# Two more blocks of the modulation matrix summed row by row during the scan, handed out with its projections

## The chip, the cores and the metric

The kernel runs on one core of a Trainium2 chip. The metric is the device time of one execution in microseconds; lower is better. Engines are named as in the profile: PE (TensorE matmuls), PEld (its weight loads), DVE (VectorE), ACT (ScalarE), POOL (GpSimd) and SP (SyncE, which here only issues DMAs). Each engine works through its own list of instructions in a fixed order, and waits at an instruction until what it needs is there.

## The reference

One layer of a diffusion trunk on 512 latent tokens and 256 context tokens, model width 2048, in float32:

```
mod  = silu(c) @ w_ada + b_ada                 # 6 x 2048 columns: sh1 sc1 gt1 sh2 sc2 gt2
p    = modulate(rms_norm(x, g_mix), sh1, sc1) @ w_in       # the context alike, with c_ctx
f    = fourier_mix(p[:, :512], w_fourier)
y    = ssd_mixer(p_ctx[:, 512:], p[:, 512:], ...)          # conv, two scans, gate, grouped norm
x    = x + gt1 * (concat(f, y) @ w_out)
x    = x + gt2 * (relu(modulate(rms_norm(x, g_mlp), sh2, sc2) @ w_mlp1)**2 @ w_mlp2)
out  = rms_norm(x, g_final)
```

The change concerns the 12288 columns of `mod`, held in the tile `mod` as 96 columns of 128 values: 0 to 15 are sh1, 16 to 31 sc1, 32 to 47 gt1, 48 to 63 sh2, 64 to 79 sc2, 80 to 95 gt2. sh2 and sc2 are needed only after the output projection.

## The kernel before, in words

Each large product keeps weights of 128 x 1024 as a tile `wraw` that is split into `whi` (ACT, rounded to the fast float format) and `wlo` (DVE, the rest), and does three matmuls for each piece (`mm3`, L106 to L108): high weights with high input, low weights with high input, high weights with low input. In the scan and the output projection `load_split` issues the load on SP (L98) and makes both halves (L99, L100), with three buffers for `wraw` and two for each half. A w_in or w_out product (`product`) has two such tiles, 48 matmuls of 512 columns.

The columns of `mod` are made in two ways.

- `ada_half` (L168 to L173): one column of 128 values from half a row at a time. A 512 KB load of transposed weights (`araw<-in_w_ada`, SP) and one multiply-and-sum over 1024 elements on DVE (L172, with a short read of the accumulator), with the conditioning vector spread over all partitions in `cl` or `clb`. Two of them for a column.
- `ada_rest` (L188 to L207): four columns, a block of 512, from rows. Eight steps; a step loads 512 KB (`araw<-in_w_adr`, L194, SP) and adds two rows of 128 x 512 to a sum `adacc` on DVE (L198 for the first, L200). After the eighth step four small matmuls (L204) sum over partitions and turn the block into columns, and DVE adds the bias (L206).

`NSB` says where the two meet: blocks 8 to `NSB` - 1 and 20 to 23 go by rows, the rest by columns. Blocks 8 to 11 are summed while the context is worked on, 20 to 23 during the MLP. Blocks 12 to `NSB` - 1 are put in the list `todo` at the scan's start (with two load buffers, pool `sbg`, and one sum, `sbg1`), and the columns from 4 x `NSB` to 79 at the output projection's start. `background(n)` does the next n steps of the list at the places where it is called:

- `scan_group` (four groups of heads) calls `background(1)` after each of its three parts; in the last group it empties the list ahead of `z_last`, which makes the last three z tiles from `w_zs`.
- `lat_group(g, nbg)` makes the five projections of a group (B, three of x, C), with `background(nbg)` after each. Projections of group g + 1 are written behind the scan of group g.
- The output projection calls `background((21 - NSB) // 2)` after each of its 16 products.

The written order is not the order on the engines: a scheduler orders the instructions of each engine when the kernel is built, by priorities and its own costs, with the weight loads at a high priority. Matmuls of a scan group therefore stand among those of the next group's projections.

At the end of the last group these steps meet. The three z tiles are gated (L586), squared and summed (L592), summed over partitions by a matmul with ones (L696), and the group's norm (L154 to L158) scales the last three outputs (L700). The other thirteen inputs of the output projection lie in DRAM; `between` reloads them through the two buffers `cvr` (L717, POOL) and splits each into `bh` (ACT, L708) and `bl` (DVE, L709). PE meanwhile does k = 0 to 12 of the first three products (their accumulators are `first`), and the last three k when the last outputs are split. `clb`, 1 MB, is loaded by POOL (L759) into memory that the scan gives back, so after the last L700.

In the output projection a product ends with an add to x (L790), a square (L771) and a sum of squares (L772), and the result goes to DRAM.

Of the kernel before, what the change touches and what calls it, by code (L numbers as in the profile page):

```python
# [30 lines left out]
NL = L // 2 + 1  # L31
SLAB_IN = 944
NZ0 = 3
NSB = 14
SHARED = [(16 + k, 0) for k in range(2, 14)]
NZ1 = 9
N1P = 3
# [17 lines left out]
def tile_hybrid_trunk(ctx, tc, xT, ctxT, cvec, ccol, vec, alog, w_ada, w_adr, w_ins, w_zs, w_in, w_dt, w_f, w_o,  # L55
# [18 lines left out]
    def acc(n=L):  # L74
        return psa.tile([P, L], F32, name="acc")[:, :n]
# [12 lines left out]
    def raw_tile():  # L88
        return pools["wp"].tile([P, HALF], F32, name="wraw")
# [20 lines left out]
    def product(ps, src, x, cuts=(8, 16)):  # L110
        k0 = 0
        nk = len(x)
        for k1 in cuts:
            w = load_split(src[:, k0:k1], (k1 - k0) * src.shape[2], src.shape[2])
            for k in range(k0, k1):
                mm3(ps, (w[0][:, k - k0], w[1][:, k - k0]), x[k], k == 0, k == nk - 1)
            k0 = k1
# [47 lines left out]
    def ada_half(pool, ch, hf, *sums):  # L165

        a = pool.tile([P, HALF], F32, name="araw")
        nc.sync.dma_start(out=a, in_=w_ada[ch if ch < 32 else ch - (4 * NSB - 32), :, hf * HALF:(hf + 1) * HALF])  # L168
        for i, (dst, half, cond) in enumerate(sums):
            o = a if i == len(sums) - 1 else pools["ws"].tile([P, HALF], F32R, name="whi").bitcast(F32)  # L170
            first, last = vcol(V_BADA + ch), half[:, ch:ch + 1]
            v.tensor_tensor_reduce(o, a, cond[:, hf * HALF:(hf + 1) * HALF], 1.0, last if hf else first,  # L172
                                   ALU.mult, ALU.add, dst[:, ch:ch + 1] if hf else last)  # L173
# [11 lines left out]
    def ada_rest(ci, pool, pool1, name="adacc"):  # L185

        held = {}

        def step(k2):
            if k2 == 0:  # L190
                held["a"] = pool1.tile([P, 512], F32, name=name)
            a = held["a"]
            w = pool.tile([P, 2, 512], F32, name="araw") if pool else raw_tile().rearrange("p (a b) -> p a b", b=512)
            nc.sync.dma_start(out=w, in_=w_adr[ci - 8 if ci < NSB else ci - 20 + NSB - 8, k2])  # L194
            for j in range(2):
                k = 2 * k2 + j
                if k == 0:
                    v.tensor_scalar(a, w[:, j], cs[:, 0:1], None, ALU.mult)  # L198
                else:
                    v.scalar_tensor_tensor(a, w[:, j], cs[:, k:k + 1], a, ALU.mult, ALU.add)  # L200
            if k2 == 7:
                pt = bank()
                for j in range(4):
                    te.matmul(pt[:, 2 * j:2 * j + 2], a[:, j * P:(j + 1) * P], ones[:, 0:2], start=True, stop=True)  # L204
                sl = slice(ci * 4, ci * 4 + 4)
                v.tensor_add(mod[:, sl], pt[:, 0:8].rearrange("p (a b) -> p a b", b=2)[:, :, 0], vt[:, sl])  # L206
        return [lambda k2=k2: step(k2) for k2 in range(8)]  # L207
# [69 lines left out]
    def background(n):  # L277
        for _ in range(min(n, len(todo))):
            todo.pop(0)()
# [183 lines left out]
    def conv(ps, t, row, o, raw):  # L463
        s.copy(raw, ps)
        ps = raw
        s.activation(o, ps, AF.Identity, bias=vcol(V_CB + t), scale=vcol(V_CW + t * 5 + 2))
        ar = o.rearrange("p (r c) -> p r c", c=row)
        pr = ps.rearrange("p (r c) -> p r c", c=row)
        for j in (0, 1, 3, 4):
            off = j - 2  # L470
            if off < 0:
                o_, i_ = ar[:, :, -off:], pr[:, :, :row + off]
            else:
                o_, i_ = ar[:, :, :row - off], pr[:, :, off:]
            v.scalar_tensor_tensor(o_, i_, vcol(V_CW + t * 5 + j), o_, ALU.mult, ALU.add)
        s.activation(o, o, AF.Silu)

    def to_tok(src, n, dst):
        pt = bank()
        for c in range(n // P):  # L480
            te.transpose(pt[:, c * P:(c + 1) * P], src[:, c * P:(c + 1) * P], ident)
        s.copy(dst, pt[:, :n].rearrange("p (c q) -> p c q", q=P))

    def lat_group(g, nbg, extra=None):
        def proj(t, o):
            ps = acc()
            product(ps, w_in[t], xm)
            conv(ps, t - T_X, 64, o, gp2.tile([P, L], F32, name="cvr"))
            background(nbg)
            return o  # L490
        bT = proj(T_B + g, gp1.tile([P, L], F32, name="bT"))
        b_tok = gp2.tile([P, NCH, P], F32, name="b_tok")
        to_tok(bT, L, b_tok)
        if extra:
            extra()
        x_tok = gp2.tile([P, NCH, HG * 64], F32, name="x_tok")
        xs_ = []
        for i in range(3):
            o = proj(T_X + g * 3 + i, gp2.tile([P, L], F32, name=f"xT{i}"))
            to_tok(o, L, x_tok[:, :, i * P:(i + 1) * P])  # L500
            xs_.append(o)
        cT = proj(T_C + g, gp2.tile([P, L], F32, name="cT"))
        return bT, b_tok, cT, xs_, x_tok

    with tc.tile_pool(name="fp", bufs=1, side="right") as fp, tc.tile_pool(name="fp2", bufs=1, side="right") as fp2:
# [6 lines left out]
        nxt = lat_group(0, 4, ctx_stats)  # L512
# [68 lines left out]
    spe = sp_stack.enter_context(tc.tile_pool(name="spe", bufs=4, side="right"))  # L581
    for ci in range(12, NSB):
        todo.extend(ada_rest(ci, sbg, sbg1))
# [136 lines left out]
    for g in range(NG):  # L720
        cur = nxt
        ys = scan_group(g, *cur)
        if g + 1 < NG:
            nxt = lat_group(g + 1, 0)
    background(len(todo))

    for i in range(3):
# [2 lines left out]
    for j in range(3):  # L730
# [3 lines left out]
        for k1 in (8, 13):  # L734
            w = load_split(w_o[j][:, k0:k1], (k1 - k0) * P, P)
            for k in range(k0, k1):
# [26 lines left out]
    todo.extend([lambda ch=ch, hf=hf: ada_half(g2p, ch, hf, (mod, half, clb))  # L763
                 for ch in range(4 * NSB, 80) for hf in range(2)])

    def sumsq(accum, x, pool, k):
        if k == 0:
            s.activation(accum, x, AF.Square)
        else:
            q = pool.tile([P, L], F32, name="nq")  # L770
            s.activation(q, x, AF.Square)  # L771
            v.tensor_add(accum, accum, q)  # L772
# [6 lines left out]
    for j in range(KT):  # L779
# [12 lines left out]
        sumsq(a1, x2, xp2, j)  # L792
        background((21 - NSB) // 2)
    v.scalar_tensor_tensor(s1, mod[:, 64:80], 1.0, vt[:, V_GMLP:V_GMLP + KT], ALU.add, ALU.mult)
# [356 lines left out]
```

## Time and profile before

| what | value |
|---|---|
| median of 3 runs | 2348.69 us (2343.1 to 2351.73) |
| profiled execution, its own time | 2345.72 us |
| its span | 2343.9 us |
| busy: PE, DVE, ACT, POOL | 2254.9, 1893.3, 1175.0, 319.9 us |
| granted PE clock, mean | 0.99 |
| bytes read from and written to HBM | 433.62 and 62.92 MB |
| loads `araw<-in_w_ada` | 164 x 512 KB, 48 of them in the output projection |
| loads `araw<-in_w_adr` | 48 x 512 KB, 16 of them in the scan (and 32 into `wraw` in the MLP) |

Times in the profile are microseconds from the start of the span, or durations. L172 is line 172 of the kernel; `acc<-bh,wlo` reads: the tile acc is written from bh and wlo. In a timeline a row has start, duration, engine, line, operation, shapes, count, and in brackets how long the engine stood idle before it and what ended that. In lists of waits a row has who waited, for whom, the total in us, how many times and the longest.

### The profile page before, as it was taken

The page shows a single profiled execution, that of the slowest core. Times are in us where ns is not written, and L with a number is a line of the kernel's source. Part 1 is how long each engine was busy: PE and PEld are TensorE (multiplying, and loading weights), DVE is VectorE, ACT ScalarE, POOL GpSimd, SP SyncE. Part 2 cuts the span into 40 slices and gives each one's busy share as a digit, 9 for nine tenths or more (in the row PEclk, how much of TensorE's full clock was granted, in tenths as well). Part 3 has the DMA queues.
Part 4 walks back from the last instruction along what each step waited for, and adds up shares of the span by engine and source line. Part 5 has one row for each costly group of instructions (what it writes and reads, how often), then busy time and mean ns, then how long its engine had stood idle before and what let it go on. Part 6 is the DMA issues. An engine that isn't in the chain of part 4 may idle for free. (4 is left out here: it accounts for less than half of the span.)

```text
span 2343.9 us, 38720 instructions
## 1 busy us (share of the span) xinstructions
PE 2254.9 (96%) x15242; PEld 1996.9 (85%) x15242; DVE 1893.3 (81%) x2580; ACT 1175.0 (50%) x1646; POOL 319.9 (14%) x346
## 2 busy tenths in 40 slices
PE   7999999999999999989999999999999999999996
PEld 2347779877777777779999999999999999999995
DVE  7978779987878767696888887777997887898778
ACT  4125335446655522264555555555765665566554
POOL 0000000000000000011122121111122222222210
PEclk9999999999999999989999999999999999999998
DMA  8988977733224399645655554444799999999993
GB/s 287 336 313 287 332 236 259 269 111 129 79 69 142 99 337 317 225 149 180 195 176 176 179 179 136 128 134 134 218 268 268 266 237 269 264 261 244 239 275 117
DMA packets 150926, 499.08 MB, mean 213 GB/s; under 512 B 17892, under 2 KB 18804, under 8 KB 150488
## 3 DMA queue, kind: packets, MB, share of 16 engines
q1 hardware_dynamic: 111448, 387.14, 48.5%
q0 software_dynamic: 38144, 107.38, 20.2%
q8 instruction: 119, 1.95, 0.3%
q10 hardware_dynamic: 1152, 2.10, 0.2%
q14 instruction: 63, 0.52, 0.1%
HBM read 433.62 MB, written 62.92 MB: 212 GB/s over the span
## 5 line engine op out<-in xcount | busy, mean ns | idle before, releaser
L85 DVE TENSOR_TENSOR wlo<-wraw,whi 128x1024 fp32r<-128x1024 f32 x427 | 552.1, 1302 | 164.7 <-ACT whi L84 161.9
L84 ACT CAST whi<-wraw 128x1024 fp32r<-128x1024 f32 x427 | 444.6, 1048 | 446.3 <-PE bank L108 161.5
L106 PE MATMUL bank<-chi,whi 128*128 128x256 f32 (+1 forms) x2000 | 569.2, 285 | 0.5 <-DVE ca L1040 0.5
L107 PE MATMUL bank<-chi,wlo 128*128 128x256 f32 (+1 forms) x2000 | 569.1, 285 | 0.1
L108 PE MATMUL bank<-clo,whi 128*128 128x256 f32 (+1 forms) x2000 | 568.8, 284 | 0.0
L106 PE MATMUL acc<-chi,whi 128*128 128x256 f32 (+1 forms) x1512 | 430.6, 286 | 7.3 <-ACT chi L830 6.7
L107 PE MATMUL acc<-chi,wlo 128*128 128x256 f32 (+1 forms) x1512 | 432.3, 286 | 5.2 <-DVE wlo L85 5.2
L108 PE MATMUL acc<-clo,whi 128*128 128x256 f32 (+1 forms) x1512 | 431.0, 285 | 0.0
L106 PEld LDWEIGHTS bank<-chi,whi 128*128 128x128 f32 x2000 | 384.1, 192 | 2.0 <-DVE ca L1040 0.7
L107 PEld LDWEIGHTS bank<-chi,wlo 128*128 128x128 f32 x2000 | 384.1, 192 | 1.6 <-DVE wlo L85 0.5
L108 PEld LDWEIGHTS bank<-clo,whi 128*128 128x128 f32 x2000 | 384.0, 192 | 1.1
L107 PE MATMUL acc<-bh,wlo 128*128 128x512 f32 x720 | 285.0, 396 | 15.8 <-DVE wlo L100 15.8
L106 PEld LDWEIGHTS acc<-chi,whi 128*128 128x128 f32 x1512 | 289.9, 192 | 9.9 <-ACT chi L830 7.9
L107 PEld LDWEIGHTS acc<-chi,wlo 128*128 128x128 f32 x1512 | 290.4, 192 | 8.5 <-DVE wlo L85 7.2
L108 PEld LDWEIGHTS acc<-clo,whi 128*128 128x128 f32 x1512 | 290.4, 192 | 1.7 <-DVE clo L832 0.6
L106 PE MATMUL acc<-bh,whi 128*128 128x512 f32 x720 | 283.9, 394 | 0.3 <-ACT whi L99 0.3
L108 PE MATMUL acc<-bl,whi 128*128 128x512 f32 x720 | 283.2, 393 | 0.0
L99 ACT CAST whi<-wraw 128x1024 fp32r<-128x1024 f32 (+2 forms) x145 | 142.8, 987 | 261.0 <-PE acc L108 227.1
L100 DVE TENSOR_TENSOR wlo<-wraw,whi 128x1024 fp32r<-128x1024 f32 (+2 forms) x145 | 165.8, 1145 | 29.0 <-ACT whi L99 28.1
L107 PEld LDWEIGHTS acc<-bh,wlo 128*128 128x128 f32 x720 | 135.4, 188 | 50.6 <-DVE wlo L100 23.0
L106 PEld LDWEIGHTS acc<-bh,whi 128*128 128x128 f32 x720 | 135.4, 188 | 28.6 <-ACT whi L99 0.7
L108 PEld LDWEIGHTS acc<-bl,whi 128*128 128x128 f32 x720 | 135.4, 188 | 27.6 <-issue 0.8
(338 smaller groups left out, 3337.6 us busy)
## 6 DMA issues: line engine op xcount, KB each, us to landing
wraw<-in_w_dram SPq DMA_DIRECT2D x276, 512.0 KB, 4.8
araw<-in_w_ada_dram SPq DMA_DIRECT2D x164, 512.0 KB, 6.9
wraw<-in_w_in_dram SPq DMA_DIRECT2D x84, 512.0 KB, 4.6
wraw<-in_w_dram POOLq DMA_DIRECT2D x64, 512.0 KB, 8.1
x<-ca POOLq DMA_DIRECT2D x112, 256.0 KB, 8.4
araw<-in_w_adr_dram SPq DMA_DIRECT2D x48, 512.0 KB, 4.6
wraw<-in_w_adr_dram SPq DMA_DIRECT2D x32, 512.0 KB, 3.6
hid<-ct POOLq DMA_DIRECT2D x32, 512.0 KB, 4.8
```

The source lines that it names most:

```text
L84: s.copy(hi, raw)
L85: v.tensor_sub(lo, raw, hi.bitcast(F32))
L99: s.copy(hi, raw)
L100: v.tensor_sub(lo, raw, hi.bitcast(F32))
L106: te.matmul(ps, a[0], b[0], start=first, stop=False, skip_group_check=on)
L107: te.matmul(ps, a[1], b[0], start=False, stop=False, skip_group_check=on)
L108: te.matmul(ps, a[0], b[1], start=False, stop=last, skip_group_check=on)
```

## The change

`NSB` goes from 14 to 16, and `lat_group` of the groups 1 to 3 is called with 1 instead of 0:

```diff
-NSB = 14
+NSB = 16
@@ for g in range(NG)
         cur = nxt
         ys = scan_group(g, *cur)
         if g + 1 < NG:
-            nxt = lat_group(g + 1, 0)
+            nxt = lat_group(g + 1, 1)
```

Blocks 14 and 15, the columns 56 to 63 of `mod` (half of sh2), are now summed from rows: 32 steps are in the list at the scan's start instead of 16, and 27 of them are called for by the groups and their projections, 5 ahead of `z_last` (12 and 4 before). The output projection has 32 sums of half a row instead of 48, and `background` gets 2 instead of 3 after each product. The host lays out the two weight arrays accordingly. In the lists of the engines PE has 8 more rows of matmuls, DVE 32 more of L198 and L200, 2 more of L206, and 16 fewer sums L172; POOL's list is the same.

The order changes from the projections of group 1 to the end of the output projection. Three places, as the program's lists have them; numbers behind names tell tiles of one name apart.

SP at the projections of the fourth group: `in_w_in` are their weights, `in_w_adr` a step's rows. Before, then now:

```order
L98 DMA wraw_5493<-in_w_in_dram 128x1024
L98 DMA wraw_5523<-in_w_in_dram 128x1024
L98 DMA wraw_5571<-in_w_in_dram 128x1024
L98 DMA wraw_5601<-in_w_in_dram 128x1024
L98 DMA wraw_5647<-in_w_in_dram 128x1024
```
```order
L98 DMA wraw_5540<-in_w_in_dram 128x1024
L194 DMA araw_5094<-in_w_adr_dram 128x1024
L98 DMA wraw_5570<-in_w_in_dram 128x1024
L194 DMA araw_5174<-in_w_adr_dram 128x1024
L98 DMA wraw_5622<-in_w_in_dram 128x1024
L194 DMA araw_5300<-in_w_adr_dram 128x1024
L98 DMA wraw_5652<-in_w_in_dram 128x1024
```

Sixteen loads of w_in stood in a row here; now nearly every one has a step's load behind it.

DVE at the end of the last group, from the add that follows the last block's matmuls (now) or from the last part's sum (before). Before, then now:

```order
L681 TENSOR_TENSOR xT2_5721<-xT2_5721,ee_6173 128x512
L586 TENSOR_TENSOR xT0_5569<-xT0_5569,zt_6481 128x512
L100 TENSOR_TENSOR wlo_6557<-wraw_6555,whi_6556 128x640
L709 TENSOR_TENSOR bl_6472<-cvr_6469,bh_6471 128x512
L709 TENSOR_TENSOR bl_6478<-cvr_6475,bh_6477 128x512
L586 TENSOR_TENSOR xT1_5645<-xT1_5645,zt_6485 128x512
L586 TENSOR_TENSOR xT2_5721<-xT2_5721,zt_6491 128x512
```
```order
L200 SCALAR_TENSOR_TENSOR adacc_6051<-araw_6276,cs_79,adacc_6051 128x512
L681 TENSOR_TENSOR xT2_5780<-xT2_5780,ee_6247 128x512
L206 TENSOR_TENSOR mod_76<-bank_6280,vt_69 128x4
L709 TENSOR_TENSOR bl_6502<-cvr_6499,bh_6501 128x512
L100 TENSOR_TENSOR wlo_6635<-wraw_6633,whi_6634 128x640
L709 TENSOR_TENSOR bl_6508<-cvr_6505,bh_6507 128x512
L586 TENSOR_TENSOR xT0_5620<-xT0_5620,zt_6559 128x512
L586 TENSOR_TENSOR xT1_5700<-xT1_5700,zt_6563 128x512
L586 TENSOR_TENSOR xT2_5780<-xT2_5780,zt_6569 128x512
L709 TENSOR_TENSOR bl_6514<-cvr_6511,bh_6513 128x512
```

Before, eleven of the thirteen reloaded inputs were split ahead of this point and the two rows here are the last; now these rows are the fourth to the sixth of thirteen, and seven more follow among the rows of the norm. The L204 that L206 reads stands on PE directly behind the last matmul of `z_last`; before, the last L204 of the scan stood among the matmuls of the last part.

DVE a little later, at the first column sum of the output projection (the operation is printed as ISA). `wlo` of 1024 and 640 columns are the two tiles of one of the first three products. Before, then now:

```order
L700 SCALAR_TENSOR_TENSOR xT2_5721<-xT2_5721,vt_69,xd0_6499 128x512
L709 TENSOR_TENSOR bl_6513<-xT0_5569,bh_6512 128x512
L709 TENSOR_TENSOR bl_6517<-xT1_5645,bh_6516 128x512
L709 TENSOR_TENSOR bl_6521<-xT2_5721,bh_6520 128x512
L100 TENSOR_TENSOR wlo_6631<-wraw_6629,whi_6630 128x1024
L172 ISA araw_6758,half_6713<-araw_6758,clb_6711,vt_69 128x1024
```
```order
L700 SCALAR_TENSOR_TENSOR xT2_5780<-xT2_5780,vt_69,xd0_6577 128x512
L709 TENSOR_TENSOR bl_6550<-cvr_6547,bh_6549 128x512
L709 TENSOR_TENSOR bl_6556<-cvr_6553,bh_6555 128x512
L709 TENSOR_TENSOR bl_6591<-xT0_5620,bh_6590 128x512
L709 TENSOR_TENSOR bl_6595<-xT1_5700,bh_6594 128x512
L709 TENSOR_TENSOR bl_6599<-xT2_5780,bh_6598 128x512
L100 TENSOR_TENSOR wlo_6687<-wraw_6685,whi_6686 128x640
L172 ISA araw_6836,half_6791<-araw_6836,clb_6789,vt_69 128x1024
L172 ISA half_6791 128x1
L100 TENSOR_TENSOR wlo_6709<-wraw_6707,whi_6708 128x1024
```

The first half of the third product's weights was split ahead of the sum that reads `clb`; now it is split behind it, and the second half of the second product's stands directly ahead.

## The prediction

> **What bounds the kernel now.** I read the page first, then the busy time of three stretches, then what the engines wait for in them. The page says that TensorE (PE) is nearly always at work.
>
> ```profile
> span 2343.9 us, 38720 instructions
> PE 2254.9 (96%) x15242; PEld 1996.9 (85%) x15242; DVE 1893.3 (81%) x2580; ACT 1175.0 (50%) x1646; POOL 319.9 (14%) x346
> ```
>
> Ends of matmuls are modelled, so 96% is no proof that PE is at its peak. What PE does unhindered shows in its starts: fifteen steps from the first to the second of these rows take 3.40 us, 0.227 us for each 512-column matmul.
>
> ```profile
> 474.14 0.39 PE L108 MATMUL acc<-bl,whi 128*128 128x512 f32 x1
> ...
> 477.54 0.39 PE L108 MATMUL acc<-bl,whi 128*128 128x512 f32 x1
> ```
>
> The change touches the scan (465 to 803 us of the span), its tail with the start of the output projection (to 840) and the rest of that projection (to 984). The columns are busy time and instructions of each engine, clock, DMA share and rate.
>
> ```profile
> core 0: us, PE busy (x) PEld busy (x) DVE busy (x) ACT busy (x) POOL busy (x), PEclk, DMA share, GB/s
> 465.00:803.00 338.00, 332.00 (x1777) 250.78 (x1776) 267.33 (x492) 184.54 (x266) 22.44 (x41) 1.00 0.33 106
> 803.00:840.00 37.00, 34.97 (x149) 27.37 (x148) 24.19 (x34) 17.77 (x26) 1.09 (x2) 1.00 0.72 249
> 840.00:984.00 144.00, 134.09 (x577) 107.17 (x578) 102.83 (x144) 32.80 (x38) 7.05 (x13) 1.00 0.88 306
> ```
>
> In the scan PE is busy 98% with DMA a third busy and VectorE (DVE) at 79%. In the output projection DMA is at 0.88 and PE loses 10 of 144 us. The waits of that stretch say to whom.
>
> ```profile
> DVE araw L172 <- DMA araw<-in_w_ada_dram: 33.3, 23, 3.3
> PEld acc L107 <- DVE wlo L100: 16.0, 14, 2.7
> PE acc L107 <- DVE wlo L100: 10.6, 11, 2.3
> ```
>
> Once in most products PE waits for wlo, the low half of a w_out tile; DVE makes it late because a column sum ahead of it in its row waits for its own load. One such place in the timeline, DVE and then PE:
>
> ```profile
> 887.85 1.29 DVE L172 CUSTOM_DVE_ANT_0 araw<-araw,clb,half 128x1024 f32<-128x1024 f32 x1 [2.42 <-DMA araw<-in_w_ada_dram]
> ...
> 892.25 1.22 DVE L100 TENSOR_TENSOR wlo<-wraw,whi 128x1024 fp32r<-128x1024 f32 x1
> ```
> ```profile
> 893.52 0.50 PE L107 MATMUL acc<-bh,wlo 128*128 128x512 f32 x1 [2.29 <-DVE wlo L100]
> ```
>
> So at most 10.6 us can be had from taking column loads out of this stage.
>
> **The change part by part.** The pieces that are exchanged cost this:
>
> ```profile
> L200 DVE SCALAR_TENSOR_TENSOR adacc<-araw,cs,adacc x30: 739/746/753, 460.6 to 749.9; 128x512 f32<-128x512 f32 x30
> ...
> L198 DVE TENSOR_SCALAR adacc<-araw,cs x2: 481/484/486, 459.8 to 697.2; 128x512 f32<-128x512 f32 x2
> ```
> ```profile
> L172 DVE CUSTOM_DVE_ANT_0 araw<-araw,clb,half 128x1024 f32<-128x1024 f32 x23 | 29.5, 1284 | 16.2 <-DMA araw<-in_w_ada_dram 15.6
> ...
> L172 DVE DVE_READ_ACCUMULATOR2_ANT mod<- 128x1 f32 x23 | 1.9, 82 | 0.0
> ```
> ```profile
> 796.92 1.05 PE L204 MATMUL bank<-ones,adacc 128*128 128x2 f32 x8
> 797.83 0.48 PE L107 MATMUL acc<-bh,wlo 128*128 128x512 f32 x1
> ```
>
> *Removed:* 16 sums of half a row, 16 x (1.284 + 0.082) = 21.9 us of DVE, with 16 loads of 512 KB. *Added in the scan:* 16 steps, 30 x 0.746 + 2 x 0.484 = 23.3 us of DVE, 16 loads of 512 KB on SP's queue, and twice the four small matmuls of L204, which hold PE for 797.83 - 796.92 = 0.91 us. Total bytes stay. POOL's queue is the same row for row, and ScalarE (ACT) has three table loads fewer, off the path with 184.54 of 338 us busy.
>
> *PE in the scan: +1.8 us*, 2 x 0.91, on the path, since PE hardly rests there.
>
> *DVE in the scan: +1 us, 0 to 6.* 267.3 + 23.3 = 290.6 of 338 us, 86%. What hides it is DVE's own idle 71 us, and the order of the changed kernel puts each added pair between rows of the scan. If a quarter of the work lacked cover, 6 us; I take 1, near the rows of the present steps, behind which PE is not seen waiting.
>
> *SP in the scan: nothing, 0 to 2.* Each added load waits for one of two buffers and w_in loads queue behind it, as the first order excerpt shows. In the changed order the wlo that needs the load behind stands at least 23 DVE rows past the one that frees the buffer, some 14 us at 0.6 us a row, while a load lands in 3.8 to 4.3 us:
>
> ```profile
> wraw<-in_w_in_dram SPq DMA_DIRECT2D x24, 512.0 KB, 3.8
> araw<-in_w_adr_dram SPq DMA_DIRECT2D x13, 512.0 KB, 4.3
> ```
>
> *The scan's tail: +11 us, 5 to 15.* This is the term that I did not look for. The last block now ends behind the z projection's last matmul: PE does its L204 there, DVE's L206 waits for it, and ten of the thirteen reload splits (L709) stand behind L206, where two stood behind the same point before (second excerpt). The reloads share two buffers:
>
> ```profile
> L717 POOL DMA_DIRECT2D cvr<-y x13: 548/548/556, 731.0 to 799.7; - x13
> L708 ACT CAST bh<-cvr x13: 609/621/633, 737.0 to 804.4; 128x512 fp32r<-128x512 f32 x13
> L709 DVE TENSOR_TENSOR bl<-cvr,bh x13: 681/684/693, 744.5 to 805.3; 128x512 fp32r<-128x512 f32 x13
> ...
> DMA to landing us min/median/max: 2.8/3.0/5.9
> ```
>
> A buffer's round is the issue 0.55, landing 3.0, cast 0.62 and split 0.68, together 4.9 us, so 2.45 us for each reload. Counted from the end of the last z matmul: L204 and L206 take 1.1; two reloads that wait in their buffers, with a split between, 2.1; eight more 19.6; then the three splits of the last outputs and the second half-split of w_out tile 1, whose rows are
>
> ```profile
> 814.31 0.83 DVE L100 TENSOR_TENSOR wlo<-wraw,whi 128x640 fp32r<-128x640 f32 x1
> ...
> 817.04 1.89 DVE L709 TENSOR_TENSOR bl<-xT,bh 128x512 fp32r<-128x512 f32 x3
> ```
>
> 1.1 + 2.1 + 19.6 + 1.9 + 0.8 = 25.5. Until that wlo PE has L204, 64 matmuls and the ones product: 0.9 + 64 x 0.227 + 0.6 = 16.0. Idle 9.5. Next, the first column sum, which waits for clb, now stands ahead of the first wlo of tile 2, where it stood behind it (third excerpt). What clb takes:
>
> ```profile
> 817.69 0.55 POOL L759 DMA_DIRECT2D clb<-cl_d  x1 [17.46 <-DVE xT L700]
> ```
> ```profile
> 826.36 1.28 DVE L172 CUSTOM_DVE_ANT_0 araw<-araw,clb,vt 128x1024 f32<-128x1024 f32 x1 [5.05 <-DMA clb<-cl_d]
> ```
>
> It is issued 0.6 us after the last L700 and there 8.7 later. That L700 stands two reloads ahead of the end: 1.1 + 2.1 + 19.6 - 4.9 + 0.7 = 18.6; with clb 27.9; with sum, read and wlo (1.28 + 0.08 + 1.22) 30.5. PE arrives at 25.5 + 14 x 0.227 = 28.7: idle 1.8. The tiles' last slices, behind two more sums, cost about 1. In all 12.3, against what PE lost here before:
>
> ```profile
> 808.96 1.12 PE L696 MATMUL bank<-qa,ones 128*128 128x512 f32 x2 [0.35 <-DVE qa L592]
> ...
> 828.09 0.50 PE L106 MATMUL acc<-bh,whi 128*128 128x512 f32 x1 [0.30 <-ACT whi L99]
> ...
> 829.31 0.50 PE L107 MATMUL acc<-bh,wlo 128*128 128x512 f32 x1 [0.71 <-DVE wlo L100]
> ```
>
> 1.4. So +11. Low end: all reloads in time, DVE's 28 rows from L206 to that wlo at 0.6 to 1.2 us make some 18.5 us; PE then idles about 3.5 there and 3 at clb: +5. High end: three reloads at the row's longest 5.9, 3 x 2.9 / 2 = 4.4 more: +15.
>
> *The output projection: -4 us, 0 to -10.6.* Of 46 sums in the window 28 are left, but the order keeps them as dense as before, four to a product for seven products, and leaves only the last products free. Waits in proportion: 10.6 x 18 / 46 = 4.1. I take this rather than the whole, as where sums remain nothing in their rows is different; more than nothing is lost nowhere, since no load is added. The windows show DMA at 0.33 in the scan and 0.88 here. The Trainium skill (Perfetto Trace Analysis, Optimization Strategy) says that regimes with different most-contended engines may gain by being interleaved; by it the whole 10.6 would be had and the sum be 7 us lower. The trace agrees on the two regimes, the order does not on the whole.
>
> *Sum:* +1.8 + 1 + 11 - 4 = +9.8 on the profiled execution's 2345.72 us: 2355.5. That execution lies 3.0 under the median of 2348.69 and within the runs' 2343.1 to 2351.73; the range bears this. 0.5% is 11.7 us, about what a measurement of this kernel can tell from no change.
>
> **Rivals.** *A, the forecast.*
>
> *B, the tail is hidden.* DVE gets through the reloads while PE still has z work, because ACT and POOL run ahead; for it speaks that before eleven of thirteen were done by then, against it that L206's place in DVE's row is fixed behind PE's last z matmul. Then +1.8 + 1 with -4 to -10.6: 2338 to 2344.5, not slower.
>
> *C, DVE becomes the scan's bound.* DVE and PE hand work to each other in each group, and DVE there often stands still for PE and then has to catch up:
>
> ```profile
> DVE xT L670 <- PE bank L667: 12.7, 10, 1.6
> ```
>
> At 86% an added pair of 1.4 us that stands just behind such a wait pushes e, hs or xd, and PE with them. Against it: in 338 us PE is busy 332. Uncovered half, 11.7 us: 2345.7 + 1.8 + 11.7 + 11 - 4 = 2366, slower; over the forecast some 3 us uncovered are enough to pass the 0.5%.
>
> *D, the waits in the output projection stay.* They come from where sums stand in DVE's row and how far ahead their buffers let them be loaded, not from how many there are, and PE loses as much on fewer products: gain 0, 2359.5. For it: a wait in nearly every product (11 in 13). Against: the last products have no sums at all. The Trainium skill (Perfetto Trace Analysis, Optimization Strategy) reads a gap that repeats on the engine that should be saturated as a possible lack of buffers; by this rule less load alone would not close it. No run here shows what more buffers do.
>
> That the steps are not handed out is no rival: the order has the 16 added loads between those of w_in, w_zs and the first w_out tiles.
>
> **How the numbers follow.** A 0.56: with all ends at once its sum would reach from -4 to +23, I give most of it +3 to +16, and a third of it lies past 11.7 us; B 0.16; C 0.13; D 0.12, two thirds past 11.7; 0.03 for a gain over 0.5%, for which no term has room. Slower by over 0.5%: 0.19 + 0.13 + 0.08 = 0.40. Within: 0.37 + 0.16 + 0.04 = 0.57. Faster: 0.03. The likeliest is 2355.5. The range 2343 to 2367 leaves out the lower half of B, the upper half of C and the edges of A, about 0.17.
>
> **What would show it.** Tail right: PE's waits between the end of the z projection and the fourth product sum to 10 us or more, most of it L107 or whi behind wlo L100, with POOL's cvr issues back to back behind L709. Wrong: under 4 us there. Output term right: DVE's wait for araw falls to some 20 us and PE's for wlo to 6 or 7, none in the last four products. Scan right: from 465 us to the last z matmul within 4 us of before. C shows as PE waits for e, hs or xd in the scan; D as 10 us of wlo waits that remain. I am wrong above all if the reloads in the tail come faster than 2.45 us each.

## The result and the profile after

| kernel | median, us | ratio to before | 95% interval |
|---|---|---|---|
| before | 2347.83 (2343.1 to 2351.73, 6 runs) | 1 | |
| after | 2363.2 (2356.14 to 2367.68, 6 runs) | 1.0059 | 1.0042 to 1.0077 |

The change made the kernel slower by 0.6%, some 14 us (0.0059 x 2347.83; 10 to 18 by the interval; the two medians lie 15.4 us apart). The profiled execution of after took 2356.14 us, 10.4 more than that of before. It is the fastest of the six runs of after, so the profile shows somewhat less than the whole loss.

The page of after, span and busy time:

```profile
span 2354.4 us, 38769 instructions
PE 2263.2 (96%) x15258; PEld 2001.3 (85%) x15258; DVE 1892.1 (80%) x2582; ACT 1172.3 (50%) x1643; POOL 320.5 (14%) x346
```

PE is busy 8.3 us more, although the change gave it only eight tiny matmuls (sixteen instructions as the profile counts them). Where that lies is found with three landmarks: the first matmul of the scan's first group (L610), the first Silu of the z projection, and the norm behind the output projection (L776). Before, then after:

```profile
471.86 1.05 PE L610 MATMUL bank<-cT,bT 128*128 128x128 f32 x8
801.82 0.60 ACT L693 ACTIVATE zt<-acc 128x512 f32<-128x512 f32 x1 [3.59 <-PE acc L108]
996.97 1.51 PE L776 MATMUL bank<-nacc,ones 128*128 128x512 f32 x2 [2.28 <-issue]
```
```profile
472.55 1.05 PE L610 MATMUL bank<-cT,bT 128*128 128x128 f32 x8
799.75 0.60 ACT L693 ACTIVATE zt<-acc 128x512 f32<-128x512 f32 x1 [1.55 <-PE acc L108]
1008.64 1.10 PE L776 MATMUL bank<-nacc,ones 128*128 128x512 f32 x2 [2.28 <-issue]
```

From L610 to the Silu 329.96 us became 327.20; from the Silu to the norm 195.15 became 208.89, 13.7 more. The second stretch, cut at 852 us, before and after (busy time of PE, PEld, DVE, ACT, POOL, then granted clock, DMA share, GB/s):

```profile
801.82:852.00 50.18, 48.15 (x207) 38.22 (x206) 32.82 (x47) 22.16 (x31) 1.64 (x3) 1.00 0.75 261
852.00:996.97 144.97, 132.79 (x572) 105.81 (x570) 99.22 (x140) 31.89 (x37) 8.24 (x16) 1.00 0.81 279
```
```profile
799.75:852.00 52.25, 43.26 (x162) 30.78 (x160) 34.68 (x53) 22.45 (x35) 6.01 (x11) 0.90 0.70 248
852.00:1008.64 156.64, 146.06 (x623) 118.40 (x624) 83.42 (x111) 34.87 (x40) 8.21 (x16) 0.98 0.64 219
```

In the tail PE stands idle 52.25 - 43.26 = 9.0 us instead of 2.0. In the rest it is idle 10.6 instead of 12.2, 1.6 less. Its busy time, though, is 8.4 us longer over both (189.3 against 180.9), of which the last block's L204 is 0.9: the same matmuls ran longer, at a granted clock of 0.90 and 0.98 where it had been 1.00. By clock, 0.10 x 52.25 = 5.2 us of that fell to the tail and 0.02 x 156.64 = 3.1 to the rest. Together that is 8.3, where 8.4 - 0.9 = 7.5 is left to divide, so this split is an estimate, good to about a microsecond. By it the tail cost some 12 us (7.0 + 5.2 = 12.2) and the output projection won 1.6 in waits and lost about 3 in clock.

The lower clock is not peculiar to this execution. The mean granted clock over the span is 0.982 to 0.987 in the six runs of after, 0.9835 on average, and 0.984 to 0.991 in the 24 runs of before that lie beside the first experiments, 0.9875 on average. Were matmuls to set the pace throughout, this would be 0.004 x 2355 = 9 us, an upper estimate of the clock's part in the loss.

What the tail waits for, in the waits of after from 801 to 860 us:

```profile
POOL cvr L717 <- DVE bl L709: 38.4, 8, 23.6
...
ACT bh L708 <- DMA cvr<-y: 12.1, 5, 5.6
...
DVE bl L709 <- ACT bh L708: 8.3, 4, 4.9
PE acc L106 <- ACT bh L708: 6.8, 5, 2.6
...
PE acc L106 <- ACT whi L99: 1.4, 3, 0.7
...
PE acc L107 <- DVE wlo L100: 0.4, 1, 0.4
```

A ring: POOL waits for a split to free a buffer, ACT for the reload, DVE for ACT, and PE for the input. Of PE's 8.9 us of waits in this window 6.8 are for `bh`, the high half of a reload, and 0.4 for `wlo`. The last issues of POOL and their landings:

```profile
803.73 0.55 POOL L717 DMA_DIRECT2D cvr<-y  x1 [23.62 <-DVE bl L709]
...
822.32 0.55 POOL L717 DMA_DIRECT2D cvr<-y  x1 [1.81 <-DVE bl L709]
823.22 0.55 POOL L759 DMA_DIRECT2D clb<-cl_d  x1 [0.35 <-issue]
```
```profile
L717 POOL DMA_DIRECT2D cvr<-y x13: 546/546/553, 735.7 to 822.3; - x13
...
DMA to landing us min/median/max: 2.8/4.1/7.0
```

Eight reloads were issued from 803.73 to 822.32, 2.66 us apart on average. Beside the last of them ran loads of x and of columns, which SP had issued from 817.86 on. DVE then:

```profile
827.59 0.69 DVE L709 TENSOR_TENSOR bl<-cvr,bh 128x512 fp32r<-128x512 f32 x1 [4.90 <-ACT bh L708]
829.78 0.69 DVE L709 TENSOR_TENSOR bl<-cvr,bh 128x512 fp32r<-128x512 f32 x1 [1.50 <-ACT bh L708]
830.39 1.89 DVE L709 TENSOR_TENSOR bl<-xT,bh 128x512 fp32r<-128x512 f32 x3
832.20 0.82 DVE L100 TENSOR_TENSOR wlo<-wraw,whi 128x640 fp32r<-128x640 f32 x1
832.93 1.28 DVE L172 CUSTOM_DVE_ANT_0 araw<-araw,clb,vt 128x1024 f32<-128x1024 f32 x1
```

In the output projection (852 to 1008 us) seven waits are left where there were ten, but up to 2.8 us long where the longest had been 2.3:

```profile
PE acc L107 <- DVE wlo L100: 8.7, 7, 2.8
```

### The profile page after: what moved, and what is told of

The parts are those of the page before. It is cut to its first block, busy times and chain, and to the rows that moved or that the text cites. A ratio compares the mean times of both kernels' runs of the same rounds, so it can differ in the third digit from the quotient of the medians.

```text
span 2354.4 us, 38769 instructions
## 1 busy us (share of the span) xinstructions
PE 2263.2 (96%) x15258; PEld 2001.3 (85%) x15258; DVE 1892.1 (80%) x2582; ACT 1172.3 (50%) x1643; POOL 320.5 (14%) x346
## 4 chain that ended last, share of the span: by engine, by line
PE 71%; DVE 12%; DMA 9%; issue 6%; ACT 1%; SPq 0%; POOL 0%; DVEq 0%; POOLq 0%; ACTq 0%
PE acc L107 12%; PE acc L108 11%; PE acc L106 11%; PE bank L106 9%; PE bank L108 9%; PE bank L107 9%; DMA araw<-in_w_ada_dram 3%; DVE araw L172 2%; DVE wlo L85 1%; PE bank L347 1%; PE bank L667 1%; DMA araw<-in_w_adr_dram 1%; DVE wlo L100 1%; PE bank L679 1%; PE bank L654 1%
```

## The experiments

In the diffs a minus line is the kernel that the run is made from (before or after, as its expectation says); three dots mark what is left out, and remarks behind # are added for the reader. Ratios are to the kernel before, in runs on the same chip.

**The output term alone.**

```diff
-                 for ch in range(4 * NSB, 80) for hf in range(2)])
+                 for ch in range(4 * NSB + 8, 80) for hf in range(2)])
-        background((21 - NSB) // 2)
+        background(2)
```

> The kernel before with the sixteen sums of the columns 56 to 63 left out of the output projection (those columns are not computed) and two steps instead of three after each product. The scan and its tail keep the order of before, so this is the output term alone. My theory, from the changed kernel's trace (waits for wlo 8.7 us against 10.6): 2 to 4 us less than before, ratio 0.998 to 0.999, DVE's wait for araw some 30 us still, PE's wlo waits 7 to 9 us. Rival D, waits stay: ratio 1.000, wlo waits 10 us. The rule by which all of it is won: 10.6 us less, ratio 0.9955.

Measured: 1.0001 (0.9989 to 1.0014). With a third of the sums gone nothing is won. The waits from 801 to 996 us:

```profile
DVE araw L172 <- DMA araw<-in_w_ada_dram: 27.5, 20, 4.0
...
PE acc L107 <- DVE wlo L100: 9.9, 10, 3.2
```

The total wait for wlo is 9.9 us against 11.3 in the same stretch of before, on fewer products and with single waits of up to 3.2. This is rival D, and not the 2 to 4 us that I expected.

**The price of scan and tail alone.**

```diff
-                 for ch in range(4 * NSB, 80) for hf in range(2)])
+                 for ch in [*range(4 * NSB, 4 * NSB + 8), *range(4 * NSB, 80)] for hf in range(2)])
-        background((21 - NSB) // 2)
+        background(3)
```

> The changed kernel with sixteen sums put back into the output projection (columns 56 to 63 are summed a second time there, and three steps follow each product as before). Scan and tail keep the order of the changed kernel, so against before this is the price of scan and tail alone. My theory: 11 to 15 us over before in the tail, minus up to 2 us in the scan, ratio 1.0045 to 1.006, and 2 to 4 us over the changed kernel. Rival D: the same as the changed kernel, 1.006. If the scan pays (rival C), last z matmul would be 5 us or more later than the 803 us of before, and it would be so here too.

Measured: 1.0044 (1.0028 to 1.0059), a hair under my range, and not 2 to 4 us above the changed kernel's 1.0059. Sixteen sums more cost nothing that the intervals show (1.0028 to 1.0059 here, 1.0042 to 1.0077 for after), the mirror of the run before. So the loss lies in scan and tail, as far as these intervals tell.

**The last block's end, moved back.**

```diff
+            if k2 == 7 and ci == NSB - 1:
+                late.append(finish)      # L204 and L206 of the last block
...
+    late.pop()()
     sp_stack.close()
```

> The changed kernel with the last block's sum over partitions (four small matmuls) and its bias add written behind the first three products. The order then has the bias add two reload splits and five rows later on DVE, and the small matmuls are no longer directly behind the last z matmul; the reload splits keep their places among the gates. My theory as refined by the trace of the changed kernel (two reload buffers at some 2.45 us a round and places behind the gates, which wait for z themselves): within 3 us of the changed kernel, 10 us or more over before, ratio 1.004 to 1.006. Rival, and what the prediction's wording says (DVE held by the bias add's wait for the small matmuls): the tail is back to that of before, ratio 1.000 or less.

Measured: 1.0056 (1.0035 to 1.0077), the same as after. The ring turns as before (801 to 860 us; its lines are numbered eight higher):

```profile
POOL cvr L725 <- DVE bl L717: 37.8, 8, 22.8
...
PE acc L106 <- ACT bh L716: 7.0, 5, 3.2
```

So L206 and its wait for the four small matmuls are not what holds the reloads.

**Two steps for each projection.**

```diff
-            nxt = lat_group(g + 1, 1)
+            nxt = lat_group(g + 1, 2)
```

> The changed kernel with two steps instead of one after each projection of the groups 1 to 3, so that the list is empty well before the last group and no block ends near the z projection; in the order eleven of thirteen reload splits then stand ahead of the last gate, and only two behind. My theory (the loss is the reloads behind the last block and the gates): tail as before, 31 to 33 us from the end of the z projection to the end of the first product instead of 46; in all 0 to 5 us less than before, ratio 0.998 to 1.000. Rival C (DVE bounds the scan once steps are dense): the scan ends 5 us or more later, ratio above 1.002. If the loss is not in the reloads' place: ratio stays 1.006.

Measured: 1.0035 (1.0017 to 1.0052). The list is empty early, and the order has eleven reload splits ahead of the last gate again. Its landmarks:

```profile
472.00 1.05 PE L610 MATMUL bank<-cT,bT 128*128 128x128 f32 x8
804.77 0.60 ACT L693 ACTIVATE zt<-acc 128x512 f32<-128x512 f32 x1
1001.59 1.10 PE L776 MATMUL bank<-nacc,ones 128*128 128x512 f32 x2 [2.28 <-issue]
```

From the Silu to the norm 196.82 us, 1.7 over before, and from the Silu to the end of the first product 33.9 (33.1 before, 47.6 in after): the tail is mended. The scan took 332.77, 2.8 over before. The whole came out slower than my 0.998 to 1.000; of the 8 us that remain by the ratio this profile accounts for 5, and the other 3 are not explained. DVE does not bound the scan even here: from 465 to 806 us PE waits 3.8 us for DVE, where it waits 2.0 before and 1.4 in after. Single profiles of the scan differ by some 3 us, though: the run with sums put back has the scan of after and took 330.91 where after took 327.20. The scan's own price is therefore settled to a few us only.

**Eight buffers for the reloads.**

```diff
-            r = gp2.tile([P, L], F32, name="cvr")
+            r = spe.tile([P, NCH, P], F32, name=f"e{k % 2}").rearrange("p a b -> p (a b)")
```

> The changed kernel with the thirteen reloads going through the eight buffers of the scan's e tiles, which are free by then, instead of through the two cvr buffers. Sixteen steps stay added and one is handed out per projection. The order then puts the last block's end ahead of the last part's rows and most reload splits behind the first gate, each 0.68 us. If two buffers with a round of 2.45 us per reload are what stretches the tail: from the first Silu of the z projection to the end of the first product 33 to 37 us (47.6 in the changed kernel, 33.1 before), POOL's issues no longer waiting for splits, ratio 1.000 to 1.004. If it is the place of the splits behind the gates alone: 42 us or more there, ratio 1.005 or more.

Measured: 1.0022 (1.001 to 1.0034); the interval lies below that of after, 0.0037 or some 9 us recovered. As expected, the order changed together with the buffers: the last block's end now stands ahead of the last part's rows. So this run does not fully separate the two buffers from the place of the splits. POOL hardly waits for splits any more (1.7 us in all, and the last issue at 807.7 instead of 822.3):

```profile
L717 POOL DMA_DIRECT2D e<-y x13: 546/546/553, 781.8 to 807.7; - x13
...
  DVE bl L709: 1.7, 1
```

The landmark that I named was missed, 45.0 us from the first Silu to the end of the first product: in this order the three z tiles end 16 us apart, so the first Silu comes early. The longest wait of PE left in its tail is 3.7 us for a w_out tile, beside DVE's wait of 4.0 for clb (797 to 852 us):

```profile
DVE araw L172 <- DMA clb<-cl_d: 4.0, 1, 4.0
...
PE acc L106 <- ACT whi L99: 3.7, 1, 3.7
```

**Earlier steps alone.**

```diff
-            nxt = lat_group(g + 1, 0)
+            nxt = lat_group(g + 1, 1)
```

> The kernel before with one step after each projection of the groups 1 to 3, and no block moved: sixteen steps, done earlier, so that the list is empty before the last group. Handing out earlier by itself costs nothing by my theory: ratio 0.999 to 1.001. Were the earlier place itself what loads the scan (the run with two steps per projection had its scan some 3 us longer), 1.001 to 1.002 with the scan 2 us or more longer.

Measured: 0.999 (0.9977 to 1.0003). By itself the change's second line costs nothing.

**More blocks alone.**

```diff
-            nxt = lat_group(g + 1, 1)
+            nxt = lat_group(g + 1, 0)
```

> The number of blocks alone: 16 as in the changed kernel, but no step after a projection of the groups 1 to 3, so that the groups call for 12 of the 32 steps and 20 stand in the list ahead of the z projection. In the order thirteen of these steps come behind the last part's add, two of them in each gap between gates and reload splits, and the last block's bias add stands directly ahead of the last norm. If the tail is priced by what stands ahead of the reloads and the norm on DVE and SP: 15 to 30 us over before, ratio 1.006 to 1.013, waits of PE for the norm and the reloads of 15 us or more. If the steps hide beside the z projection (33 us of PE): ratio 1.000 to 1.004.

Measured: 1.0149 (1.0126 to 1.0173), past my upper end, some 35 us. From 800 to 870 us PE waits for the last block's sum, whose loads come one behind the other:

```profile
PE bank L204 <- DVE adacc L200: 15.3, 1, 15.3
DVE adacc L200 <- DMA araw<-in_w_adr_dram: 10.7, 7, 2.9
...
PE acc L106 <- ACT bh L708: 7.0, 2, 5.1
```

So of the loss that the change's first line brings alone, the second line gave back more than half.

**Why the output projection's waits stay.** Two buffers were tried on the kernel before: a third pair for the split weights, and a fifth for the sums' loads.

```diff
+            if third:                                     # load_split, output projection only
+                third.append(third[0] if len(third) % 3 == 0 else ws)
+                ws = third[-1]
...
+    third.append(g2_stack.enter_context(tc.tile_pool(name="wx", bufs=1, side="right")))
```

> The kernel before with a third pair of buffers for the split weights in the output projection, in memory that the scan has given back; all 48 sums stay. By D (the waits come from where a sum stands ahead of a split and from how little ahead the two pairs of split buffers let ACT and DVE work): PE's waits for wlo in the output projection fall from 11 to 5 us or less, ratio 0.995 to 0.998. If DMA sets the pace of that stage (share 0.88), the waits stay or move to whi behind its load, ratio 0.999 to 1.001.

Measured: 0.9978 (0.9966 to 0.999). Its profiled execution took 2347.75 us against a median of 2344.27, so its profile is read for the waits and not for the time.

```diff
-    g2p = g2_stack.enter_context(tc.tile_pool(name="g2", bufs=4, side="right"))
+    g2p = g2_stack.enter_context(tc.tile_pool(name="g2", bufs=5, side="right"))
```

> The kernel before with five buffers instead of four for the half rows of the column sums and for x in the output projection. The order of all engines is the same; only loads can be issued earlier. If a sum's wait for its own load is what delays wlo and a buffer more brings the load forward: DVE's wait for araw falls from 33 to 20 us or less, PE's for wlo from 11 to 7, ratio 0.998. If the loads are issued behind others in SP's queue and not held by their buffers: nothing, ratio 0.9995 to 1.0005.

Measured: 0.9999 (0.9987 to 1.0011). The waits for wlo from 852 us to the norm, with the third pair and then with the fifth load buffer (9.9 in 10 before; the third pair's kernel has its lines four higher):

```profile
PE acc L111 <- DVE wlo L104: 4.7, 3, 2.1
```
```profile
PE acc L107 <- DVE wlo L100: 11.1, 9, 2.9
```

DVE's wait for araw is 30.6 us with the third pair (840 to 984 us; 33.3 before); PE feels little of it. The loads are not held by their buffers. What is short is how far ACT and DVE may split ahead of PE.

**Both repairs on the changed kernel, and the better kernel.**

> The changed kernel with both repairs: the reloads through eight buffers (1.0022 so far by itself) and a third pair of split buffers in the output projection (0.9978 by itself on the kernel before). If the two act in different places and add: ratio 0.999 to 1.001. If with fewer sums the third pair wins more than with all (all waits for wlo go): 0.996 to 0.998, and then moving the sums pays once the buffers are there.

The edits are those of the eight reload buffers and the third pair. Measured: 1.0009 (0.9995 to 1.0023). Within the interval the two repairs add, and the third pair wins no more on fewer sums.

> The kernel before with one step after each projection of the groups 1 to 3 (0.9990 by itself) and the third pair of split buffers (0.9978 by itself), no block moved. Sum of the two: ratio 0.996 to 0.998, faster than both kernels; if it is slower than the version with the blocks moved and both repairs, the moved sums have a worth of their own.

The edits are `lat_group(g + 1, 1)` and the third pair, on the kernel before. Measured: 0.997 (0.9954 to 0.9986), 2339.43 us. It is faster than both kernels, and its interval lies below that of the changed kernel with both repairs. PE from the first Silu to 852 us and on to the norm:

```profile
802.13:852.00 49.87, 47.73 (x204) 37.57 (x203) 29.79 (x41) 21.79 (x31) 1.63 (x3) 1.00 0.77 266
852.00:991.65 139.65, 133.83 (x574) 108.27 (x573) 100.71 (x142) 30.50 (x37) 8.23 (x16) 0.99 0.83 292
```

Idle time behind 852 us is 5.8 instead of 12.2, with all 48 sums in place: the waits that the change was to thin out go by a buffer, and moving the sums has no worth of its own that these runs show. The changed kernel with both repairs still loses about 9 us against this one. A part of it goes with the clock: its runs have a mean granted clock of 0.9857, those of this kernel 0.9883, and 0.0026 x 2343 = 6 us is an upper estimate of that part. What lowers the clock there was not tested.

## Why the prediction was right and where it was wrong

- *The sum.* 2355.5 for the profiled execution, 2356.14 measured; the median, 2363.2, is inside the range but beyond the 11.7 us up to which I called it no change, which had the larger chance (0.57 against 0.40). That the profile meets the forecast to 0.6 us is luck twice over. The profiled execution lies 7 us under the median of after, and in the profiled pair two errors cancel: the scan came out 5.6 us under its terms (-2.8 for +2.8), the output projection 5.5 over its own (+1.5 for -4). (All upper ends together make +24.8, and not the +23 given for A, which leaves out SP's 2.)
- *Scan: +1.8 (PE), +1 (DVE), 0 (SP).* The profile of after has the stretch 2.8 us shorter, the run with two steps per projection 2.8 longer, and two runs with the same scan differ by 3. The last z matmul ends at 801.1 us instead of about 803, within the 4 us named as the sign. Neither confirmed nor refuted beyond that. Rival C needed 11.7 us of uncovered DVE work; PE's waits for DVE in the scans looked at are 3.8 us at most.
- *The scan's tail: +11, 5 to 15.* The stage was right, and so in sum was the size, some 12; the way there was not. The step had PE idle 9.5 us at the wlo of tile 1 and 1.8 behind clb, and its sign was 10 us or more of waits, most of it behind wlo. PE waited 8.9 us, which is between this sign and the 4 us that would have refuted it, and 6.8 of them reload by reload for bh, 0.4 for wlo. Net of before the idle time is 7.0 for the forecast 11; what fills the size up is a lower granted clock, about 5 us, for which the sum had no term. That these two make 12 is luck. The slow reloads themselves came as forecast: issues 2.66 us apart for the 2.45 of the step, although a reload took 4.1 us in the middle to land and not 3.0, and the wlo of tile 1 started 31 us after the last z matmul (801.1), where the step had it end after 25.5. DVE did not wait for clb, which landed at 832.9, just as the late splits were done. Rival B is out.
- *"DVE's L206 waits for it, and ten of the thirteen reload splits (L709) stand behind L206".* This was the wrong holder. With L206 moved away the time stays; with eight buffers some 9 of the 14 us go, and with an earlier end of the list the tail is mended. The two buffers, and splits that the scheduler put among the gates behind the z projection, make the ring; how much each of the two weighs was not separated.
- *The output projection: -4, 0 to -10.6.* The step that failed is "Waits in proportion", 10.6 x 18 / 46. A third fewer sums give 0.0001 (-0.0011 to 0.0014), -2.6 to +3.3 us. The last products are free of waits as forecast, but the others keep theirs, fewer and longer (8.7 us where I gave 6 or 7; DVE's wait for araw 31.8 where I gave 20), and the clock is lower there. The reading under it, that a sum's wait for its own load makes wlo late, does not hold alone: with a third pair of split buffers DVE waits for the loads as before, and PE's waits for wlo fall from 9.9 to 4.7 us. Rival D, with 0.12, was the right one here, and the full 10.6 by interleaving the two regimes was furthest off.
- The reading of the repeating gap as a lack of buffers (the Trainium skill, Perfetto Trace Analysis, Optimization Strategy) holds in these runs for the split weights (0.9978) and not for the sums' loads (0.9999).

## What to carry to other kernels

A wait that repeated in nearly every product depended here on which buffer was short, and not on how much work stood around it. Take away a buffer's limit before moving work, and try both neighbours: here one buffer gave 0.2% and the other nothing. When a list of background work is made longer, look at where it ends, and whether something with few buffers is ordered among its last steps. And read the granted clock beside the idle time: in the tail of after it was some 5 of 12 us.

## What the runs showed of the hardware

The granted clock fell to half after some short stalls, but not after all, and also without any. In the output projection of after, PE rows around one wait:

```profile
902.83 0.39 PE L106 MATMUL acc<-bh,whi 128*128 128x512 f32 x1
905.85 0.80 PE L107 MATMUL acc<-bh,wlo 128*128 128x512 f32 x1 [2.64 <-DVE wlo L100]
906.44 0.63 PE L108 MATMUL acc<-bl,whi 128*128 128x512 f32 x1
...
908.15 0.63 PE L106 MATMUL acc<-bh,whi 128*128 128x512 f32 x1
908.58 0.48 PE L107 MATMUL acc<-bh,wlo 128*128 128x512 f32 x1
908.89 0.39 PE L108 MATMUL acc<-bl,whi 128*128 128x512 f32 x1
```

Matmuls that start 0.227 us apart before the wait start 0.43 apart behind it, for 2.7 us: six steps took 2.73 instead of 1.36, so with the 2.64 us wait came 1.4 us more. No fixed threshold shows. Before had a wait of 2.29 us at 893.52 without it, the run with sums put back one of 2.96 at 829.14 and the run with two steps one of 3.35 at 937.76, while in the fastest kernel it followed one of 2.15:

```profile
965.76 0.50 PE L111 MATMUL acc<-bh,wlo 128*128 128x512 f32 x1 [2.15 <-DVE wlo L104]
...
968.45 0.63 PE L110 MATMUL acc<-bh,whi 128*128 128x512 f32 x1
968.88 0.63 PE L111 MATMUL acc<-bh,wlo 128*128 128x512 f32 x1
```

In the run with sums put back the same half clock begins in the middle of the scan, where PE waits for nothing from 600 to 620 us:

```profile
608.86 0.57 PE L656 MATMUL bank<-sel,pch 112*128 112x512 f32 x1
609.23 0.63 PE L106 MATMUL acc<-bh,whi 128*128 128x512 f32 x1
609.66 0.63 PE L107 MATMUL acc<-bh,wlo 128*128 128x512 f32 x1
```

The Trainium skill (TensorE: Matmul & The Clock Gate, What's actually happening) describes a gate that halves the array's clock after an idle window of about 3.4 us and opens it after about as long of work, in windows that run free of the program. These rows agree on the half and on a moment that varies; the idle time that sufficed here was shorter, and at 609 us there was none. That the fewer but longer waits of after lose in clock what they win in idle time is read from the profile of after (1.6 won, about 3 lost). No run separates the two, and what set off the half clock without a stall stays open.
